# Gate columns of the expert layer: operands from VectorE and ScalarE alone, with more lag

## The chip, the cores and the metric

The kernel runs on one core of a Trainium2 chip. The metric is the device time of one execution in microseconds (us); lower is better. The engines are called as in the profile: PE is TensorE (matrix products), PEld its loading of stationary operands, DVE is VectorE, ACT is ScalarE, POOL is GpSimd, and SP starts DMA transfers.

## The reference

One encoder block over 1024 tokens of width 1024. A normalized input is projected to the queries, keys and values of a differential attention with 4 heads, to a short convolution, and to two gates; the gated sum is projected back and added to the input. Then comes a feed-forward layer over 16384 tiny experts, and a last normalization:

```
def chunk(xc):                       # PEER, product keys over 128 x 128 experts
    sc = einsum(q, sub_keys)         # 8 heads x 2 halves x 128 keys
    s1, i1 = top_k(sc[:, :, 0], 16); s2, i2 = top_k(sc[:, :, 1], 16)
    top, pos = top_k(all sums s1 + s2, 16)
    eidx = i1 * 128 + i2 at pos;  g = softmax(top)
    a = gelu(einsum(expert_u[eidx], xc))
    return einsum(g * a, expert_v[eidx])
```

So each token picks 8 x 16 = 128 experts, with a weight for each.

## The kernel before, in words

The tokens are 8 tiles of 128. Tiles 0 to 4 (group 0) meet all experts densely: PE multiplies every expert's `u` by the tokens, ACT applies gelu, DVE multiplies by a gate that is zero for experts not picked, and PE multiplies by `v`. Tiles 5 to 7 (group 1) fetch only the picked rows by indirect DMA (L739), and DVE works on them (L746, L755) beside the dense part.

The order of the program is: the projections of all tiles, then attention, gates and outputs of group 0, the key scores of group 0, and then the same stages (convolution, attention, mixing, scores) for group 1. Then comes the dense part over 128 blocks of 128 experts.

Two generators run beside the stages of group 1. The main program calls `tick(us)` after each group of matmuls with a rough time of its own; each generator then takes a step whenever its budget is used up (1.5 us of that time for `select_gen_all`, 1.6 us for `weights_gen`). So their instructions are spread among those of the main program, in the queue of each engine, at places that the program text fixes; a planner then orders the instructions of each engine by modelled times.

`select_gen` does the top-16 searches on DVE for one tile, twice (4 heads each). To read the picked key's index it compares positions with an iota (L637, DVE), multiplies the 0/1 result by the f32 indices `sf` (L639, POOL) and sums (L640, DVE).

`weights_gen` turns the picks of a tile of group 0 into dense gates. After three transposes the 128 picks lie on the 128 partitions, one token per column: `ib` holds the two key indices, `w` the weights. The gates of a token are then one matmul of two 128 x 128 one-hot matrices over the picks. A step handles WQ = 4 tokens: DVE compares the two indices with an iota in one instruction (`ms`, L714), POOL multiplies the first half by the weights into `o1` (L718), ACT casts the second half into `o2` (L720), PE multiplies (four matmuls with f32 operands, L695), and ACT copies the result into `wbuf` (L696). The operands lie in memory as [partition, token, key] and are written in the order key, token, so neighbours in the order of writing are 512 bytes apart. Each tile has 4 blocks of 8 steps; a block goes to DRAM in one transfer (`w_d`, L726). In all there are 160 steps and 20 transfers. The matmuls of a step are issued one step after its operands, but at the end of each block right behind them (L725). `ms`, `o1` and `o2` have WFB = 2 buffers. The results use two PSUM banks; the pool of these banks changes once, when the scores of group 0 are done.

The dense part reads the gates back (`wt`), so it needs all of `w_d` (`drain(wgt)`, L881). `mix` normalizes the rows of a group with a ring of `nt + MIXW` row buffers (`mixw`).

Of the kernel before, what the change touches and what calls it, by code (L numbers as in the profile page):

```python
# [49 lines left out]
WB = 4  # L50
WT = 32
WQ = 4
WFB = 2
GATHER = 2.0
SEL_STEP = 1.5
SEL_STEP_D = 8
# [9 lines left out]
def block_kernel(ctx, tc, x, wqkv, wcols, wpr, wo, wq, skT, uv, uT, an_w, fn_w, fin_w, sub_w,  # L66
# [7 lines left out]
    def pool(name, bufs=1, stack=None, **kw):  # L74
        return (stack or left).enter_context(tc.tile_pool(name=name, bufs=bufs, **kw))
# [448 lines left out]
    def mix(tt0, nt, c0, keep_hn, rings, mT, hnT, outer=None):  # L524
        with ExitStack() as st:
            if outer:
                st = outer
            wk = pool("mixw", nt + MIXW, stack=st)
            fn_b = rows_bcast(pool("mixn", stack=st), fn_w, D, "fn_b")
            xts = []  # L530
            for i in range(nt):
                tt = tt0 + i
                xts.append(row(wk, "xt2"))
                SP.dma_start(out=xts[i], in_=x[tt * P:(tt + 1) * P, :])
            later = []
            for j in range(2):
                w = units_k(rings[j], wo, j)
                for i in range(nt):
                    tt, xt = tt0 + i, xts[i]
                    ph = ps["g"].tile([P, 512], F32, name="ph2", tag="g")  # L540
                    gemm(ph, kts(mT, slice(c0 + i * P, c0 + (i + 1) * P)), w)
                    V.tensor_add(xt[:, j * 512:(j + 1) * 512], ph, xt[:, j * 512:(j + 1) * 512])
                    if j == 1:
                        SP.dma_start(out=h_d[tt * P:(tt + 1) * P, :], in_=xt)
                        hn = row(wk, "hn")
                        norm_rows(xt, fn_b, hn, hn, "h")
                        if keep_hn:
                            SP.dma_start(out=hn_d[tt * P:(tt + 1) * P, :], in_=hn)
                        if later:
                            transposes(*later.pop(0))  # L550
                        later.append((hn, hnT, c0 + i * P))
            if outer:
                return lambda: transposes(*later.pop(0))
            transposes(*later.pop(0))
# [39 lines left out]
    def select_gen(small, tt, ev, gw, done=None):  # L594
        hh = PH // 2
        sh = [P, hh, TOPK, TOPK]
        s3 = [P, hh, TOPK]

        t = small

        for a in range(2):
            sc = t([P, PH, NK], F32, "sc")
            SP.dma_start(out=sc, in_=sc_d[tt * P:(tt + 1) * P, a * PH * NK:(a + 1) * PH * NK]
                         .rearrange("p (h c) -> p h c", c=NK))
            sv, si = t([P, PH, TOPK], F32, "sv"), t([P, PH, TOPK], U32, "si")
            for hp in range(PH):
                top16(t, sc[:, hp, :], NK, sv[:, hp, :], si[:, hp, :])
                yield
            ohs = sc.rearrange("p h c -> p (h c)").bitcast(BF16).rearrange("p (j h a k) -> p j h a k", j=2, a=TOPK, k=TOPK)
            sf = t([P, PH, TOPK], F32, "sf")  # L610
            V.tensor_copy(out=sf, in_=si)
            svv = sv.rearrange("p (h q) k -> p h q k", q=2)
            sfv = sf.rearrange("p (h q) k -> p h q k", q=2)
            tv, ti = t(s3, F32, "tv"), t(s3, U32, "ti")
            cd = t([P, hh, CAND], F32, "cd")
            for c0, a0, na, nb in ((0, 0, 4, TOPK), (64, 4, TOPK - 4, 4)):
                sc2 = [P, hh, na, nb]
                V.tensor_tensor(out=cd[:, :, c0:c0 + na * nb].rearrange("p h (a b) -> p h a b", b=nb),
                                in0=svv[:, :, 0, a0:a0 + na].unsqueeze(3).broadcast_to(sc2),
                                in1=svv[:, :, 1, :nb].unsqueeze(2).broadcast_to(sc2), op=ALU.add)  # L620
            yield
            for h in range(hh):
                top16(t, cd[:, h, :], CAND, tv[:, h, :], ti[:, h, :])
                yield
            for j in range(2):
                pi, pj, pf = t(s3, U32, "pi"), t(s3, U32, "pj"), t(s3, BF16, "pf")
                if j == 0:
                    V.tensor_scalar(pi, ti, 4, None, op0=ALU.logical_shift_right)
                    V.tensor_scalar(pj, ti, 2, None, op0=ALU.logical_shift_right)
                    V.scalar_tensor_tensor(pf, pj, -12.0, pi, op0=ALU.add, op1=ALU.max)  # L630
                else:
                    V.tensor_scalar(pi, ti, 12, None, op0=ALU.bitwise_and)
                    V.tensor_scalar(pj, ti, 3, None, op0=ALU.bitwise_and)
                    V.scalar_tensor_tensor(pf, ti, 64.0, pi, op0=ALU.is_lt, op1=ALU.mult)
                    V.tensor_tensor(out=pf, in0=pf, in1=pj, op=ALU.add)
                oh = ohs[:, j]
                V.tensor_tensor(out=oh, in0=pf.unsqueeze(2).broadcast_to(sh), in1=iota_k.unsqueeze(1).broadcast_to(sh),  # L637
                                op=ALU.is_equal)
                PL.tensor_tensor(out=oh, in0=oh, in1=sfv[:, :, j, :].unsqueeze(3).broadcast_to(sh), op=ALU.mult)  # L639
                V.tensor_reduce(out=ev[j][:, a * 64:(a + 1) * 64].rearrange("p (h k) -> p h k", k=TOPK),  # L640
                                in_=oh.rearrange("p h a k -> p h k a"), axis=AX.X, op=ALU.add)
                yield
            dv = t(s3, F32, "dv")
            V.tensor_tensor(out=dv, in0=tv, in1=tv[:, :, 0:1].broadcast_to(s3), op=ALU.subtract)
            A.activation(tv, dv, AF.Exp)
            zz = t([P, hh], F32, "zz")
            V.tensor_reduce(out=zz, in_=tv, axis=AX.X, op=ALU.add)
            V.reciprocal(out=zz, in_=zz)
            V.tensor_tensor(out=gw[:, a * 64:(a + 1) * 64].rearrange("p (h k) -> p h k", k=TOPK), in0=tv,
                            in1=zz.unsqueeze(2).broadcast_to(s3), op=ALU.mult)  # L650
            if done:
                done(a * 64, (a + 1) * 64)
            yield
# [30 lines left out]
        yield from select_gen(t, tt, ev, gw, done)  # L684

    def weights_gen(wf):
        later = []
        iota_t = wf.tile([P, NK, WQ], BF16, name="iota_t", tag="iota_t", bufs=1)
        repeated_iota(wf, iota_t, "wtr")

        def finish(buf, q, o1, o2):
            for t in range(0, WQ, 4):
                pw = ps["w"].tile([P, 4, NK], F32, name="pw", tag="g")
                for u in range(4):
                    PE.matmul(pw[:, u, :], lhsT=o2[:, t + u, :], rhs=o1[:, t + u, :], start=True, stop=True)  # L695
                A.copy(out=buf[:, :, q + t:q + t + 4], in_=pw.rearrange("p t i -> p i t"))  # L696

        for c in range(NB):
            while c >= len(chosen):
                yield  # L700
# [5 lines left out]
            w = wf.tile([P, P], F32, name="wtr", tag="wtr", bufs=2)  # L706
            A.copy(out=w, in_=pt[:, 2, :])
            for b in range(P // WT):
                buf = wf.tile([P, NK, WT], F32, name="wbuf", tag="wbuf", bufs=1)
                for q in range(0, WT, WQ):  # L710
                    ts = slice(b * WT + q, b * WT + q + WQ)
                    sh = [P, NK, WQ]
                    ms = wf.tile([P, 2] + sh[1:], BF16, name="ms", tag="ms")
                    V.tensor_tensor(out=ms, in0=ib[:, :, ts].unsqueeze(2).broadcast_to([P, 2] + sh[1:]),  # L714
                                    in1=iota_t.unsqueeze(1).broadcast_to([P, 2] + sh[1:]), op=ALU.is_equal)
                    o1 = wf.tile([P, WQ, NK], F32, name="o1", tag="o1")
                    o2 = wf.tile([P, WQ, NK], F32, name="o2", tag="o2")
                    PL.tensor_tensor(out=o1.rearrange("p t i -> p i t"), in0=ms[:, 0],  # L718
                                     in1=w[:, ts].unsqueeze(1).broadcast_to(sh), op=ALU.mult)
                    A.copy(out=o2.rearrange("p t i -> p i t"), in_=ms[:, 1])  # L720
                    if later:
                        finish(*later.pop(0))
                    later.append((buf, q, o1, o2))
                    yield
                finish(*later.pop(0))  # L725
                A.dma_start(out=w_d[c * (P // WT) + b], in_=buf)  # L726

    def gather_gen(gat):
        st = {}
# [95 lines left out]
    with ExitStack() as pb:  # L825
# [7 lines left out]
        with ExitStack() as st:  # L833
# [18 lines left out]
            cfg.update(raw=raw, lo=PL)  # L852
            scores(2, NB - 2, 2 * P, (wring, wloc), hnT, sk)
            ready.update(range(2, NB))

    pa = ExitStack()
    ctx.push(pa)
# [185 lines left out]
```

## Time and profile before

| | |
|---|---|
| Runs (us) | 3186.97, 3195.77, 3201.72; median 3195.77 |
| The profiled execution | 3191.78 us, its span 3190.0 us |
| Mean granted TensorE clock | 0.978 |
| Busy over the span | PE 94%, PEld 87%, DVE 83%, ACT 41%, POOL 29% |
| Instructions | 45907 |
| Costliest groups | dense matmuls L905, indirect fetches L739, DVE on fetched rows L746 and L755 |
| L718 (POOL, `o1`) | 160 times, 203.0 us in all |

Times are from the profile of one execution. A group of instructions is shown with its line, engine, operation, the tiles it writes and reads, shapes, count, total and mean time, and then the idle time of the engine just before, with what ended it. Matmuls overlap each other, so their durations add up to more than the time that passes. A wait for several things is put down to the one that came last.

### The profile page before, as it was taken

To read this page: it belongs to the slowest core of one execution; us is meant where nothing else is said; L and a number is where in the kernel's file an instruction comes from. 1 tells how busy PE (TensorE), PEld (TensorE's weight loads), DVE (VectorE), ACT (ScalarE), POOL (GpSimd) and SP (SyncE) were. 2 spreads that over 40 slices of the span, in tenths; PEclk is the share of its full clock that TensorE was granted. 3 is DMA by queue.
4 is the path that set the end of the run, shared out by engine and by line. 5 is a ranking of instruction groups with operands and counts; after the bars stand their busy time and mean duration, and the time that the engine had idled before them with its cause. 6 is when DMAs were issued, how large, how long until landed. Compare 5 with 4: busy or idle time off the path is not lost.

```text
span 3190.0 us, 45907 instructions
## 1 busy us (share of the span) xinstructions
PE 3012.1 (94%) x17551; PEld 2761.0 (87%) x17551; DVE 2646.3 (83%) x4665; ACT 1302.9 (41%) x2344; POOL 923.5 (29%) x716
## 2 busy tenths in 40 slices
PE   7999999898989879799999999999999999999994
PEld 6799998798988869789989989899889999999993
DVE  5442466378999996799999999999999999999898
ACT  3322364335567766533333333333333333333332
POOL 2310000035344444223222222223332323333333
PEclk9999999999999989899999999999999999999997
DMA  5451232555444375779878888888889999898887
GB/s 180 145 182 67 83 113 80 199 172 213 146 172 157 144 260 196 255 249 333 316 277 321 316 299 309 295 316 293 313 328 343 340 341 348 326 347 325 328 336 281
DMA packets 237549, 801.11 MB, mean 251 GB/s; under 512 B 18832, under 2 KB 123280, under 8 KB 174096
## 3 DMA queue, kind: packets, MB, share of 16 engines
q0 software_dynamic: 64704, 442.53, 37.5%
q1 hardware_dynamic: 152592, 305.30, 27.8%
q10 hardware_dynamic: 20032, 50.34, 4.1%
q8 instruction: 138, 2.26, 0.3%
q14 instruction: 83, 0.68, 0.1%
HBM read 714.74 MB, written 83.36 MB: 250 GB/s over the span
## 4 chain that ended last, share of the span: by engine, by line
PE 56%; DVE 17%; issue 11%; DMA 8%; POOL 4%; ACT 3%; SPq 0%; ACTq 0%; POOLq 0%; DVEq 0%
PE z L905 17%; PE pout L905 10%; PE held L905 6%; PE pq L228 4%; PE pg L228 4%; POOL uvt L739 3%; PE ph L228 3%; DMA uvt<-in_uv,idx 3%; DVE acc L755 2%; PE py L228 2%; PE pw L695 2%; DVE uvt L746 2%; DVE ms L714 1%; PE pv L228 1%; PE pk L228 1%
## 5 line engine op out<-in xcount | busy, mean ns | idle before, releaser
L739 POOL DMA_INDIRECT uvt<-in_uv,idx x384 | 528.1, 1375 | 1288.5 <-DVE acc L755 1011.0
L905 PE MATMUL z<-actTh,uh 128*128 128x320 f32 x2048 | 636.3, 311 | 5.5 <-ACT pr L929 4.5
L905 PE MATMUL z<-actTh,uhl 128*128 128x320 f32 x2048 | 636.5, 311 | 1.1 <-DVE uhl L898 1.1
L905 PE MATMUL z<-actTl,uh 128*128 128x320 f32 x2048 | 635.3, 310 | 0.0
L746 DVE SCALAR_TENSOR_TENSOR uvt<-uvt,hng 128x1024 f32<-128x1024 f32 x384 | 468.0, 1220 | 41.1 <-DMA uvt<-in_uv,idx 40.3
L755 DVE SCALAR_TENSOR_TENSOR acc<-uvt,wt,acc 128x1024 f32<-128x1024 f32 x381 | 487.8, 1280 | 1.3 <-ACT wt L749 1.2
L905 PEld LDWEIGHTS z<-actTh,uh 128*128 128x128 f32 x2048 | 386.0, 188 | 20.5 <-ACT pr L929 8.6
L905 PEld LDWEIGHTS z<-actTl,uh 128*128 128x128 f32 x2048 | 386.2, 189 | 10.1
L905 PEld LDWEIGHTS z<-actTh,uhl 128*128 128x128 f32 x2048 | 386.8, 189 | 8.5 <-DVE uhl L898 2.2
L905 PE MATMUL pout<-vh,ph 128*128 128x512 f32 x768 | 302.5, 394 | 23.2 <-ACT ph L896 15.0
L905 PE MATMUL pout<-vhl,ph 128*128 128x512 f32 x768 | 301.1, 393 | 0.0
L905 PE MATMUL pout<-vh,phl 128*128 128x512 f32 x768 | 300.5, 391 | 0.0
L718 POOL TENSOR_TENSOR o<-ms,wtr 128x512 f32<-128x512 bf16 x160 | 203.0, 1311 | 262.1 <-PE pw L695 123.4
L748 ACT ACTIVATE wt<-zt 128x1 f32<-128x1 f32 x384 | 77.0, 201 | 493.3 <-DVE uvt L746 493.0
L957 DVE TENSOR_TENSOR hacc<-pout,hacc 128x512 f32<-128x512 f32 x384 | 259.4, 681 | 19.6 <-PE pout L905 19.1
L185 DVE TENSOR_TENSOR wl<-wr,wh 128x2048 fp32r<-128x2048 f32 x66 | 157.9, 2392 | 117.7 <-ACT wh L184 117.7
L896 ACT CAST uh<-raw 128x1024 fp32r<-128x1024 f32 x128 | 134.3, 1049 | 193.5 <-DMA raw<-in_uT 187.9
L184 ACT CAST wh<-wr 128x2048 fp32r<-128x2048 f32 x74 | 141.0, 1907 | 168.9 <-DMA wr<-in_wq 31.6
L695 PE MATMUL pw<-o,o 128*128 128x128 f32 x1280 | 169.1, 284 | 41.2 <-POOL o L718 17.6
L695 PEld LDWEIGHTS pw<-o,o 128*128 128x128 f32 x1280 | 161.1, 198 | 49.3 <-issue 25.6
L905 PE MATMUL held<-vhl,ph 128*128 128x512 f32 x512 | 199.6, 391 | 0.0
L720 ACT CAST o<-ms 128x512 f32<-128x512 bf16 x160 | 179.6, 1138 | 38.8 <-DVE ms L714 26.0
(290 smaller groups left out, 6673.5 us busy)
## 6 DMA issues: line engine op xcount, KB each, us to landing
raw<-in_uT SPq DMA_DIRECT2D x128, 512.0 KB
raw<-in_uv SPq DMA_DIRECT2D x128, 512.0 KB
w_d<-wbuf ACTq DMA_DIRECT2D x20, 2048.0 KB
wt<-w_d SPq DMA_DIRECT2D x32, 1280.0 KB
wr<-in_wcols SPq DMA_DIRECT2D x28, 1024.0 KB
wr<-in_wq SPq DMA_DIRECT2D x24, 1024.0 KB
xt<-in_x SPq DMA_DIRECT2D x16, 512.0 KB
q_d<-qt POOLq DMA_DIRECT2D x32, 256.0 KB
```

The source lines that it names most:

```text
L184: A.copy(out=op[0][sl], in_=src)
L185: lo.tensor_sub(op[1][sl], src, op[0][sl].bitcast(F32))
L228: PE.matmul(pd, lhsT=l[a], rhs=r[b], start=i == 0 and j == 0, stop=i == n - 1 and j == len(c) - 1)
L695: PE.matmul(pw[:, u, :], lhsT=o2[:, t + u, :], rhs=o1[:, t + u, :], start=True, stop=True)
L718: PL.tensor_tensor(out=o1.rearrange("p t i -> p i t"), in0=ms[:, 0], in1=w[:, ts].unsqueeze(1).broadcast_to(sh), op=ALU.mult)
L720: A.copy(out=o2.rearrange("p t i -> p i t"), in_=ms[:, 1])
L739: PL.indirect_dma_start(out=t[:], out_offset=None, in_=uv, in_offset=bass.IndirectOffsetOnAxis(ap=sels[c][1][:, k:k + 1], axis=0))
L746: V.scalar_tensor_tensor(u, u, 1.0, st[c], op0=ALU.mult, op1=ALU.mult, accum_out=zt)
L755: V.scalar_tensor_tensor(st["acc"], v, wt, st["acc"], op0=ALU.mult, op1=ALU.add)
L896: A.copy(out=hi, in_=t)
L905: PE.matmul(ps, lhsT=lhs[k][a], rhs=rhs[k][b], start=first and k == 0 and j == 0, stop=last and k == n - 1 and j == 2)
L957: V.tensor_add(hacc[:, t - NR, ds], ps, hacc[:, t - NR, ds])
```

## The change

- `weights_gen` makes each comparison by itself. `ms` is now the first comparison alone (DVE, bf16). The second comparison is written by DVE straight into `o2` (f32, in the key, token order). `o1` is made by ACT: four activations per step, one per token, each reading every fourth element of `ms` and multiplying by the weight of the pick as a per-partition scale. POOL has no part in it.
- `ms`, `o1` and `o2` have three buffers (WFB = 3).
- The matmuls of a step come two steps behind its operands (`made`), and the copy out of a result one more step behind (`done`). `flush()` finishes what is pending: after each tile, and once when the pool of PSUM banks changes.
- In `select_gen` the product with the indices goes to DVE, with `sf` in bf16.
- The second `mix` (group 1) has one row buffer less (2 instead of MIXW = 3 beside the tiles' own).

```
-WFB = 2
+WFB = 3
...
-            wk = pool("mixw", nt + MIXW, stack=st)
+            wk = pool("mixw", nt + (2 if tt0 else MIXW), stack=st)
...
-            sf = t([P, PH, TOPK], F32, "sf")
+            sf = t([P, PH, TOPK], BF16, "sf")
...
-                PL.tensor_tensor(out=oh, in0=oh, in1=sfv[:, :, j, :].unsqueeze(3).broadcast_to(sh), op=ALU.mult)
+                V.tensor_tensor(out=oh, in0=oh, in1=sfv[:, :, j, :].unsqueeze(3).broadcast_to(sh), op=ALU.mult)
...
+        def operands(c, b, q, ib, w):
+            ts = slice(b * WT + q, b * WT + q + WQ)
+            ms = wf.tile(sh, BF16, name="ms", tag="ms")
+            V.tensor_tensor(out=ms, in0=ib[:, 0, ts].unsqueeze(1).broadcast_to(sh), in1=iota_t, op=ALU.is_equal)
+            o2 = wf.tile([P, WQ, NK], F32, name="o2", tag="o2")
+            V.tensor_tensor(out=o2.rearrange("p t i -> p i t"), in0=ib[:, 1, ts].unsqueeze(1).broadcast_to(sh),
+                            in1=iota_t, op=ALU.is_equal)
+            o1 = wf.tile([P, WQ, NK], F32, name="o1", tag="o1")
+            for u in range(WQ):
+                A.activation(o1[:, u, :], ms[:, :, u], AF.Copy, scale=w[:, b * WT + q + u:b * WT + q + u + 1])
+            made.append((c, b, q, o1, o2))
+
+        def columns():
+            c, b, q, o1, o2 = made.pop(0)
+            pw = ps["w"].tile([P, WQ, NK], F32, name="pw", tag="g")
+            for u in range(WQ):
+                PE.matmul(pw[:, u, :], lhsT=o2[:, u, :], rhs=o1[:, u, :], start=True, stop=True)
+            done.append((c, b, q, pw))
+
+        def keep():
+            c, b, q, pw = done.pop(0)
+            if q == 0:
+                at["buf"] = wf.tile([P, NK, WT], F32, name="wbuf", tag="wbuf", bufs=1)
+            A.copy(out=at["buf"][:, :, q:q + WQ], in_=pw.rearrange("p t i -> p i t"))
+            if q == WT - WQ:
+                A.dma_start(out=w_d[c * (P // WT) + b], in_=at["buf"])
+
+        def flush():
+            while done:
+                keep()
+            while made:
+                columns()
+                keep()
...
                 for q in range(0, WT, WQ):
-                    ms = wf.tile([P, 2] + sh[1:], BF16, name="ms", tag="ms")
-                    V.tensor_tensor(out=ms, in0=ib[:, :, ts].unsqueeze(2).broadcast_to([P, 2] + sh[1:]),
-                                    in1=iota_t.unsqueeze(1).broadcast_to([P, 2] + sh[1:]), op=ALU.is_equal)
-                    PL.tensor_tensor(out=o1.rearrange("p t i -> p i t"), in0=ms[:, 0],
-                                     in1=w[:, ts].unsqueeze(1).broadcast_to(sh), op=ALU.mult)
-                    A.copy(out=o2.rearrange("p t i -> p i t"), in_=ms[:, 1])
-                    if later:
-                        finish(*later.pop(0))
-                    later.append((buf, q, o1, o2))
+                    operands(c, b, q, ib, w)
+                    if done:
+                        keep()
+                    if len(made) > 2:
+                        columns()
                     yield
-                finish(*later.pop(0))
-                A.dma_start(out=w_d[c * (P // WT) + b], in_=buf)
+            flush()
...
             scores(2, NB - 2, 2 * P, (wring, wloc), hnT, sk)
             ready.update(range(2, NB))
+            state["flush"]()
```

## Rows read from the trace of the kernel before

The columns of a row of groups: line, engine, operation, tile written <- tiles read, shapes, count | busy us, mean ns of one | idle time before, and what ended it.

**Rows 1.** The page, part 1: busy us (share of the span) x instructions.

```profile
PE 3012.1 (94%) x17551; PEld 2761.0 (87%) x17551; DVE 2646.3 (83%) x4665; ACT 1302.9 (41%) x2344; POOL 923.5 (29%) x716
```

**Rows 2.** Stretches: length, busy us (x instructions) by engine, granted clock, DMA share, GB/s.

```profile
700.00:800.00 100.00, 87.69 (x545) 86.01 (x544) 87.75 (x286) 53.46 (x75) 56.52 (x31) 0.93 0.53 186
800.00:1200.00 400.00, 351.66 (x2237) 329.51 (x2236) 379.08 (x971) 267.67 (x397) 169.35 (x133) 0.95 0.49 179
1000.00:1100.00 100.00, 88.92 (x596) 83.04 (x595) 97.28 (x243) 75.87 (x133) 40.23 (x34) 0.95 0.42 157
1200.00:1320.00 120.00, 115.80 (x798) 113.94 (x797) 83.92 (x194) 83.21 (x120) 49.92 (x39) 1.00 0.49 175
1320.00:3150.00 1830.00, 1797.12 (x9971) 1627.17 (x9969) 1723.77 (x2605) 626.74 (x1289) 544.45 (x392) 1.00 0.88 319
```

**Rows 3.** Stretches, line L714 (DVE) alone, then line L639 (POOL) alone.

```profile
800.00:1200.00 400.00, 81.40 (x106) 0.95 0.49 179
...
800.00:1200.00 400.00, 24.01 (x12) 0.95 0.49 179
700.00:1320.00 620.00, 40.08 (x20) 0.96 0.50 180
```

**Rows 4.** Waits of PE, 800 to 1200: total us, times, longest.

```profile
PE pw L695 <- POOL o L718: 11.7, 10, 2.0
PE pw L695 <- ACT wbuf L696: 10.9, 3, 9.2
...
PE pw L695 <- ACT o L720: 5.8, 7, 3.0
```

**Rows 5.** Timeline near 1006 us: start, us, engine, line.

```profile
1005.95 2.38 POOL L639 TENSOR_TENSOR sc<-sc,sf 128x1024 bf16<-128x1024 bf16 x1 [3.75 <-DVE rz L395]
...
1006.45 1.88 DVE L396 SCALAR_TENSOR_TENSOR rz<-rz,nlam,zs 128x1 f32<-128x1 f32 x1
```

**Rows 6.** Groups by form, DVE, 800 to 1200.

```profile
L714 DVE TENSOR_TENSOR ms<-ib,iota_t 128x1024 bf16<-128x1024 bf16 x106 | 82.4, 787 | 4.0 <-ACT o L720 2.9 <-POOL o L718 1.0
L185 DVE TENSOR_TENSOR wl<-wr,wh 128x2048 fp32r<-128x2048 f32 x22 | 56.1, 2548 | 6.5 <-ACT wh L184 6.5
...
L640 DVE TENSOR_REDUCE e<-sc 128x64 f32<-128x1024 bf16 x12 | 25.0, 2088 | 0.0
L397 DVE SCALAR_TENSOR_TENSOR p<-p,rz,p 128x1024 f32<-128x1024 f32 x12 | 18.1, 1507 | 0.1
...
L637 DVE TENSOR_TENSOR sc<-pf,iota_k 128x1024 bf16<-128x1024 bf16 x12 | 8.2, 679 | 0.1
...
L396 DVE SCALAR_TENSOR_TENSOR rz<-rz,nlam,zs 128x1 f32<-128x1 f32 x12 | 6.5, 538 | 0.0
```

**Rows 7.** Single lines, whole run: count, ns min/median/max, first and last start.

```profile
L714 DVE TENSOR_TENSOR ms<-ib,iota_t x160: 654/679/2030, 732.6 to 1313.4; 128x1024 bf16<-128x1024 bf16 x160
...
L185 DVE TENSOR_TENSOR wl<-wr,wh x66: 2268/2291/3779, 11.4 to 1287.6; 128x2048 fp32r<-128x2048 f32 x66
...
L397 DVE SCALAR_TENSOR_TENSOR p<-p,rz,p x32: 1259/1284/2124, 358.7 to 1082.0; 128x1024 f32<-128x1024 f32 x32
...
L396 DVE SCALAR_TENSOR_TENSOR rz<-rz,nlam,zs x32: 191/219/1916, 358.4 to 1080.1; 128x1 f32<-128x1 f32 x32
```

**Rows 8.** Groups by form, whole run, DVE and ACT.

```profile
L957 DVE TENSOR_TENSOR hacc<-pout,hacc 128x512 f32<-128x512 f32 x384 | 259.4, 681 | 19.6 <-PE pout L905 19.1
...
L720 ACT CAST o<-ms 128x512 f32<-128x512 bf16 x160 | 179.6, 1138 | 38.8 <-DVE ms L714 26.0 <-PE pw L695 9.2 <-issue 2.2
...
L196 ACT COPY dT<-pt 128x512 f32<-128x512 f32 x64 | 37.2, 592 | 10.8 <-PE pt L191 10.7
...
L449 ACT ACTIVATE at<-po,rz 128x128 f32<-128x128 f32 x32 | 12.0, 374 | 29.1 <-PE po L228 29.1
```

**Rows 9.** Timeline at 1290 us, DVE.

```profile
1290.10 1.28 DVE L714 TENSOR_TENSOR ms<-ib,iota_t 128x1024 bf16<-128x1024 bf16 x2
```

**Rows 10.** Chain that ended last, near 1328 us: start, us, what.

```profile
1328.05 19.98 DMA wt<-w_d
```

More of the change, by code (lines that the diff above doesn't have):

```diff
@@ L686, in weights_gen @@
     def weights_gen(wf):
-        later = []
         iota_t = wf.tile([P, NK, WQ], BF16, name="iota_t", tag="iota_t", bufs=1)
         repeated_iota(wf, iota_t, "wtr")
[L691 to L696, printed above, removed]
+        made, done, at = [], [], {}
+        sh = [P, NK, WQ]
+        def operands(c, b, q, ib, w):
[28 more added lines that the diff above has]
+                keep()
+        state["flush"] = flush
         for c in range(NB):
@@ L708, in weights_gen @@
             for b in range(P // WT):
-                buf = wf.tile([P, NK, WT], F32, name="wbuf", tag="wbuf", bufs=1)
                 for q in range(0, WT, WQ):
-                    ts = slice(b * WT + q, b * WT + q + WQ)
-                    sh = [P, NK, WQ]
-                    ms = wf.tile([P, 2] + sh[1:], BF16, name="ms", tag="ms")
-                    V.tensor_tensor(out=ms, in0=ib[:, :, ts].unsqueeze(2).broadcast_to([P, 2] + sh[1:]),
-                                    in1=iota_t.unsqueeze(1).broadcast_to([P, 2] + sh[1:]), op=ALU.is_equal)
-                    o1 = wf.tile([P, WQ, NK], F32, name="o1", tag="o1")
-                    o2 = wf.tile([P, WQ, NK], F32, name="o2", tag="o2")
-                    PL.tensor_tensor(out=o1.rearrange("p t i -> p i t"), in0=ms[:, 0],
-                                     in1=w[:, ts].unsqueeze(1).broadcast_to(sh), op=ALU.mult)
-                    A.copy(out=o2.rearrange("p t i -> p i t"), in_=ms[:, 1])
-                    if later:
-                        finish(*later.pop(0))
-                    later.append((buf, q, o1, o2))
+                    operands(c, b, q, ib, w)
[3 more added lines that the diff above has]
+                        columns()
                     yield
-                finish(*later.pop(0))
-                A.dma_start(out=w_d[c * (P // WT) + b], in_=buf)
+            flush()
     def gather_gen(gat):
```

## The prediction

> **What bounds the kernel now.** I read the busy line of the page first: PE is busy for 94% of the span, DVE for 83%, and one would call the kernel PE-bound [rows 1]. The change touches only part of the span, so the next view is the table of stretches [rows 2]. From 1320 to 3150 us (the dense part) PE is busy for 1797 of 1830 us and sets the pace. The comparisons of the gate columns start between 733 and 1313 us [rows 7], and there it is otherwise: from 800 to 1200 us DVE is busy for 379.1 of 400 us and PE for 351.7, at a mean granted clock of 0.95; in the hundred us from 1000 DVE reaches 97.28%. From 700 to 800 us DVE has 12 us to spare, from 1200 to 1320 us 36 us. So the stretch from 800 to 1200 decides, and in it DVE, not PE, is the fuller engine. Of the 160 steps (a step makes four gate columns) 106 lie there, and 12 of the POOL products of the selection [rows 3].
>
> The waits of PE in that stretch name the gate columns all the same: PE stands 28.4 us before their matmuls, 11.7 for POOL's `o1`, 10.9 for ACT's copy out and 5.8 for ACT's `o2` [rows 4]. These are what the change takes away. But POOL and ACT start when DVE's `ms` is there, so a wait for `o1` can be a DVE that is behind.
>
> **What DVE gets back.** POOL's products hold DVE up. At 1006 us a DVE operation on one element takes 1.88 us beside a POOL product of 2.38 us [rows 5]; its median is 0.219. I compare the means in the stretch [rows 6] with the medians of the whole run, which are mostly undisturbed [rows 7]: L714 106 x (0.787 - 0.679) = 11.4 us, L185 22 x (2.548 - 2.291) = 5.7, L396 12 x (0.538 - 0.219) = 3.8, L397 12 x (1.507 - 1.284) = 2.7; 24 us. The many smaller forms of that list, taken the same way, bring it to about 49 us. With L718 and L639 gone from POOL I credit 49, with 24 and 55 as ends.
>
> **What DVE is given, per step.** Now: one comparison of 1024 bf16, 0.679 undisturbed. After: two of 512. The bf16 one (`ms`) keeps the fixed part, which the one-element operation bounds at 0.19 [rows 7], and half the rest: 0.19 + (0.679 - 0.19) / 2 = 0.43 us. The other writes `o2` as f32 in the layout of the matmul, each element 512 bytes from the last. No DVE operation of this trace writes so. Below, the f32 addition of 512 elements takes 0.681 (L957). Above, ACT's cast L720, which writes exactly this pattern today, takes 1.138 where an ACT copy of 512 elements into contiguous places takes 0.592 (L196), a factor of 1.92 [rows 8]; on 0.681 that is 1.31. The nearest DVE row is the reduction L640, which reads its 1024 elements 32 bytes apart: 2.088, so 1.04 for 512 if all of it scales, 1.14 if 0.19 is fixed [rows 6]. I take 1.10. Neighbours overlap by 0.08: two L714 together take 1.28, not 1.36 [rows 9]. So a step costs DVE 0.43 + 1.10 - 0.08 - 0.679 = 0.77 us more, and 106 steps 82 us.
>
> [...]
>
> **Selection.** The product L639 goes from POOL to DVE: 12 in the stretch. One operand is repeated along the innermost index, which no row shows. [...] I take the dearer one: 12 x (1.284 - 0.08) = 14 us (below: 7). [...]
>
> **ACT.** One cast of 1.138 becomes four activations of 128 elements with a scale from SBUF; L449 is one, 0.374 [rows 8], so 1.50, 0.36 more. 106 x 0.36 = 38 us on 267.7 busy us of 400 [rows 2]: hidden as long as ACT is not full. Reading `ms` at every fourth element could cost as the strided write does, (1.138 - 0.592) / 512 = 1.07 ns an element, 0.55 a step, 58 us more: still below 440. On ACT's queue the copies out and the casts of weights stand behind these four; the extra step of lag covers that.
>
> **PE, buffers, DMAs.** The matmuls are as many and as long. Two more steps of lag and a third buffer let operands come later; the forced catch-up after every eighth step (20 times) becomes one after every 32nd (5) and one where the first PSUM pool closes. The transfers to `w_d` are the same 20 on ACT's queue. One row buffer less in the second mix: the third `hn` waits for the transposes of the first, which stand before it in PE's order; nothing (if it did wait, it would be for those transposes, a few us, once).
>
> **The sum.** From 800 to 1200 us DVE would be busy for 379.1 + 82 + 14 - 49 = 426 us. At the share that it reaches in its best hundred us, 0.973, that is 438 us: 38 more. PE's 28 us of waits are not saved there: the same PE work stands before a later DVE, and the waits move to the softmax maximum and to the columns. Outside it, the other 54 steps and 8 selection products add 42 + 10 us, less some 24 us of POOL's disturbance, to stretches with 48 us to spare; PE's waits for columns end there: 6 us gained (12 to -5). In the dense part the products of the three other token tiles, 4 each, add 12 x 1.2 = 14 us to a DVE with 106 us idle behind a PE with 33: nothing (if the cover fails, 14). At its start the first gate block is read back in 19.98 us [rows 10] after the last write; the last step's operands come about 2 us later (0.77 of DVE, 0.36 of ACT, two more copies out). Sum: 38 - 6 + 2 = 34 us. The profiled execution took 3191.8 us (its span 3190.0), so 3226; the median of the runs shown is 4 us above that execution: **3230 us**.
>
> **Rivals.**
> - *DVE writes `o2` at full rate (0.681).* [...] Place: the same stretch. 379 + 106 x (0.681 - 0.33) + 7 - 49 = 374 us of DVE, 385 us at 0.973, 15 saved, and 8 elsewhere: **3173**, faster. It decides from `o2` below 0.79 us, where the stretch with the other terms comes out even.
> - *Everything at its dear end.* `o2` at 1.31, only 24 us given back: 379 + 104 + 14 - 24 = 473, 486 us at 0.973, 86 more: **3282**. ACT's strided reads push the same way. For it: ACT shows just this write at this price.
> - *The bound doesn't move.* DVE's queue is full of work that PE needs only later (selection, columns two steps ahead), so the excess is worked off in the 36 idle us from 1200 to 1320 and PE keeps its pace: **3196**. Against: the softmax maxima L387 and the weights' low parts L185 stand in the same in-order queue.
>
> **Chances.** My forecast 0.44 (own range 3205 to 3255), the dear end 0.18, full-rate writes 0.22, no movement 0.16. The spread of the runs (3187 to 3202) allows 0.5%, 16 us, to be told from nothing. Faster is the full-rate case, 0.22; the same is the unmoved bound, 0.16; slower the rest, 0.62. Range: from just below 3173, the middle of the fast case, to just above the dear one: 3172 to 3285.
>
> **What would show it.** `o2` as a DVE group of 160 at about 1.1 us and `ms` at 0.43; L639 at about 1.28 on DVE; L396 back at 0.22; no DVE operation stretched beside POOL; no PE waits for `o1`. The stage from 700 to the first dense matmul would be some 34 us longer with DVE at 95% or more of its middle, and the dense part as long as before. I am wrong if `o2` takes less than 0.8, or if DVE falls below 90% there while the stage doesn't shrink (then ACT or the lag sets the pace).

## The result, and the profile after

The changed kernel takes 3236.34 us, median of four runs (3234.53 to 3238.88), beside 3198.74 us for the kernel before on the same chip (3186.97 to 3202.25): a ratio of 1.0128, 95% interval 1.0106 to 1.0150. The forecast was 3230 us. So it is slower, by 38 us, and the profiled execution is 46 us longer (its span 3236.2 us against 3190.0). Direction and size were right; several of the places were not, so the size is in part luck.

**The groups.** First the new or moved instructions, from 700 to 1400 us of the changed kernel (line, engine, operation, shapes, count | busy us, mean ns of one | idle before).

```profile
L697 DVE TENSOR_TENSOR o<-ib,iota_t 128x512 f32<-128x512 bf16 x160 | 168.9, 1069 | 12.9 <-PE pw L708 12.9
L695 DVE TENSOR_TENSOR ms<-ib,iota_t 128x512 bf16<-128x512 bf16 x160 | 74.2, 470 | 2.0 <-ACT o L701 1.8
L639 DVE TENSOR_TENSOR sc<-sc,sf 128x1024 bf16<-128x1024 bf16 x22 | 26.6, 1211 | 0.1
L397 DVE SCALAR_TENSOR_TENSOR p<-p,rz,p 128x1024 f32<-128x1024 f32 x12 | 15.4, 1280 | 0.0
L396 DVE SCALAR_TENSOR_TENSOR rz<-rz,nlam,zs 128x1 f32<-128x1 f32 x12 | 2.5, 211 | 0.0
```

```profile
L701 ACT ACTIVATE o<-ms,wtr 128x128 f32<-128x128 bf16 x640 | 208.7, 404 | 70.3 <-PE pw L708 46.0 <-DVE ms L695 22.3 <-PE ps L376 1.2
L715 ACT COPY wbuf<-pw 128x512 f32<-128x512 f32 x160 | 89.9, 577 | 29.0 <-DMA w_d<-wbuf 15.5 <-PE pw L708 13.4
```

On DVE the price list of the forecast held to within 0.07 us: `o2` 1.069 us (forecast 1.10), `ms` 0.470 (0.43), the selection product 1.211 (1.28), and the two rows that measured POOL's disturbance of DVE are back at their undisturbed times, L396 from 538 to 211 ns and L397 from 1507 to 1280 ns [rows 6]. The four activations cost ACT 1.62 us a step (forecast 1.50).

**The stretches** of the changed kernel (columns as in [rows 2]):

```profile
700.00:800.00 100.00, 77.43 (x462) 74.37 (x460) 87.83 (x266) 45.73 (x104) 21.49 (x7) 0.91 0.40 141
800.00:1200.00 400.00, 353.54 (x2188) 332.04 (x2189) 387.19 (x1048) 276.42 (x676) 9.52 (x12) 0.94 0.45 165
1000.00:1100.00 100.00, 85.07 (x578) 78.66 (x577) 99.54 (x231) 83.31 (x217) 5.78 (x7) 0.98 0.41 153
1200.00:1320.00 120.00, 105.12 (x667) 101.98 (x666) 103.69 (x240) 82.53 (x200) 2.59 (x3) 0.91 0.57 207
1320.00:1400.00 80.00, 57.47 (x321) 54.40 (x320) 72.73 (x240) 40.68 (x100) 4.32 (x4) 0.74 0.55 201
1400.00:3150.00 1750.00, 1743.97 (x9718) 1587.15 (x9717) 1648.67 (x2437) 602.04 (x1246) 516.52 (x366) 1.00 0.89 321
```

DVE's share from 800 to 1200 rose from 379.1 to 387.2 us, and to 99.5% in its best hundred [rows 2]. But PE was busy for 353.5 us there, against 351.7 before, with 2188 matmul records against 2237 [rows 2]: it lost little. It fell back where no loss was forecast: 77.4 against 87.7 us from 700 to 800, and 57.5 us of the 80 from 1320. ACT, at 276.4 of 400, was never full.

**The landmarks.** The same three lines of PE in both kernels, before first, then after (ns min/median/max, first and last start us): the transposes of the picks, the key scores, the first form of the dense matmuls.

```profile
L703 PE MATMUL ptw<-ident,e x15: 270/272/332, 722.2 to 1215.9; 128*128 128x128 f32 x15
L564 PE MATMUL pcs<-sk,qp x256: 270/275/579, 618.5 to 1314.1; 128*128 128x128 f32 x128
L905 PE MATMUL z<-actTh,uh x2048: 302/310/415, 1317.7 to 3122.7; 128*128 128x320 f32 x187
```

```profile
L732 PE MATMUL ptw<-ident,e x15: 272/273/477, 732.0 to 1267.9; 128*128 128x128 f32 x15
L564 PE MATMUL pcs<-sk,qp x256: 270/275/582, 617.4 to 1344.4; 128*128 128x128 f32 x128
L925 PE MATMUL z<-actTh,uh x2048: 302/310/637, 1380.7 to 3167.2; 128*128 128x320 f32 x187
```

Differences of these starts give the account of the 46 us: +10 when the first picks are transposed, before a single step; +30 at the last key score; +63 at the first dense matmul; +45 at the last one (3122.7 to 3167.2). So 10 us are lost ahead of the steps, 20 in the steps' stretch, 33 between the last score and the dense part, and 18 come back in the dense part, whose start no longer waits for its inputs (before, PE stood 15.0 us at one of its first `pout` matmuls, for ACT's `ph`). How the 53 us between the first picks and the dense part split at the last score is a matter of order, not of cause: kernel 3 below has its last score at 1318.1 us, only 4 us later than before, and its first dense matmul at 1380.5 all the same.

**The tail.** PE of the changed kernel after the last scores (start, us, engine, line, [idle before <- releaser]):

```profile
1342.88 1.16 PE L708 MATMUL pw<-o,o 128*128 128x128 f32 x8 [0.53 <-ACT wbuf L715]
1343.88 0.83 PE L564 MATMUL pcs<-sk,qp 128*128 128x128 f32 x6
...
1352.65 2.08 PE L708 MATMUL pw<-o,o 128*128 128x128 f32 x8 [0.56 <-ACT wbuf L715]
1366.31 3.78 PE L708 MATMUL pw<-o,o 128*128 128x128 f32 x16 [11.58 <-ACT wbuf L715]
...
1377.93 2.04 PE L708 MATMUL pw<-o,o 128*128 128x128 f32 x8 [1.09 <-DVE sv L591]
1380.65 0.64 PE L925 MATMUL z<-actTh,uh 128*128 128x320 f32 x1 [0.68 <-ACT wbuf L715]
```

and what ACT did in the longest of these waits:

```profile
1353.39 1.37 ACT L701 ACTIVATE o<-ms,wtr 128x128 f32<-128x128 bf16 x4
1363.54 1.04 ACT L916 CAST vh<-raw 128x1024 fp32r<-128x1024 f32 x1 [8.77 <-DMA raw<-in_uv]
1364.49 1.30 ACT L701 ACTIVATE o<-ms,wtr 128x128 f32<-128x128 bf16 x4
```

When the scores are done, ten steps are still open, and they end one after the other with nothing else for PE to do. In the middle ACT stands 8.77 us at a cast for the dense part whose transfer isn't there; the copy out and the activations of the next steps are queued behind it, and PE waits 11.58 us. The granted clock of these 80 us is 0.74 on the mean: 1.00 from 1320 to 1342 us, but 0.50 from 1352.6 to 1370.1, and eight matmuls take 2.08 us at 1352.65, where they took 1.16 at 1342.88. What lowered it isn't shown. The tail shows where the delay comes out, not what makes it: kernel 1 below, which loses nothing, has one too, 32 us from its last score to its first dense matmul, with a wait of 10.83 us for the same copy.

**PE's waits** of the changed kernel from 700 to 1400 us (total, times, longest):

```profile
PE pw L708 <- ACT wbuf L715: 44.8, 28, 11.6
PE pw L708 <- DVE o L697: 12.6, 8, 4.5
PE ptw L732 <- DVE e L640: 11.2, 2, 10.4
```

The waits for POOL's `o1` and ACT's `o2` of [rows 4] are gone, and the waits for the columns as a whole rose: in this longer stretch from 41.2 us to 63.7 (the idle time of the matmul group in either kernel). That the name is now the copy out does not say that the copy is the cause; the experiments had to.

### The profile page after: what moved, and what is told of

The parts are those of the page before. It is cut to its first block, busy times and chain, and to the rows that moved or that the text cites. A ratio compares the mean times of both kernels' runs of the same rounds, so it can differ in the third digit from the quotient of the medians.

```text
span 3236.2 us, 46187 instructions
## 1 busy us (share of the span) xinstructions
PE 3035.4 (94%) x17551; PEld 2786.4 (86%) x17551; DVE 2711.6 (84%) x4857; ACT 1331.8 (41%) x2822; POOL 672.8 (21%) x524
## 4 chain that ended last, share of the span: by engine, by line
PE 50%; DVE 21%; issue 15%; DMA 6%; POOL 6%; ACT 2%; SPq 0%; POOLq 0%; DVEq 0%; ACTq 0%
PE z L925 15%; PE pout L925 8%; PE held L925 6%; POOL uvt L758 6%; PE pq L228 4%; PE pg L228 4%; DVE o L697 3%; DMA uvt<-in_uv,idx 2%; PE py L228 2%; DVE wl L185 2%; PE ph L228 2%; DVE ms L695 1%; PE pv L228 1%; DVE e L640 1%; DMA wr<-in_wq 1%
## 5 line engine op out<-in xcount | busy, mean ns | idle before, releaser
L758 POOL DMA_INDIRECT uvt<-in_uv,idx x384 | 542.1, 1412 | 1446.8 <-DVE acc L774 961.5
L185 DVE TENSOR_TENSOR wl<-wr,wh 128x2048 fp32r<-128x2048 f32 x66 | 150.8, 2286 | 114.0 <-ACT wh L184 112.9
L708 PE MATMUL pw<-o,o 128*128 128x128 f32 x1280 | 186.3, 297 | 63.7 <-ACT wbuf L715 44.8
L708 PEld LDWEIGHTS pw<-o,o 128*128 128x128 f32 x1280 | 174.0, 208 | 77.0 <-ACT wbuf L715 58.6
L701 ACT ACTIVATE o<-ms,wtr 128x128 f32<-128x128 bf16 x640 | 208.7, 404 | 70.3 <-PE pw L708 46.0
L949 ACT ACTIVATE pr<-z 128x640 f32<-128x640 f32 x128 | 90.2, 704 | 341.1 <-PE z L925 314.4
L916 ACT CAST vh<-raw 128x1024 fp32r<-128x1024 f32 x128 | 130.1, 1047 | 165.2 <-PE pout L925 156.4
```

Source lines behind the costliest of these rows:

```text
L185: lo.tensor_sub(op[1][sl], src, op[0][sl].bitcast(F32))
L701: A.activation(o1[:, u, :], ms[:, :, u], AF.Copy, scale=w[:, b * WT + q + u:b * WT + q + u + 1])
L708: PE.matmul(pw[:, u, :], lhsT=o2[:, u, :], rhs=o1[:, u, :], start=True, stop=True)
L758: PL.indirect_dma_start(out=t[:], out_offset=None, in_=uv, in_offset=bass.IndirectOffsetOnAxis(ap=sels[c][1][:, k:k + 1], axis=0))
L916: A.copy(out=hi, in_=t)
```

## The experiments

Two theories at the start. **Load:** DVE has more work than before in the stretch that sets the end, so the time follows DVE's microseconds. **Coupling** (called lag in the later runs): the columns two steps behind and the copy one more make PE, ACT and the two PSUM banks wait for each other. Ratios are to the kernel before on the same chip, with 95% intervals; the numbers follow the labels (there is no 9). Diffs are to the changed kernel, those of 6 and 11 to the kernel before. None of the twelve is faster than the kernel before.

**1. The same number of elements, written side by side.** Only the access order of `o2` changes; the matmuls then read another arrangement, so this kernel does not make the right gates.

```
-V.tensor_tensor(out=o2.rearrange("p t i -> p i t"), ...
+V.tensor_tensor(out=o2.rearrange("p t i -> p (t i)").rearrange("p (i t) -> p i t", t=WQ), ...
```

> The changed kernel, with one thing altered: the second comparison writes its 512 f32 results one behind the other and not 512 bytes apart (same count, type, reader and tile; so the matmuls read another arrangement, and the gates are not the reference's). Theory load (DVE has too much work): L697 falls from 1.07 to about 0.68 us, 160 x 0.39 = 62 us of DVE vanish between 700 and 1380 us, and most of the 41 us lost comes back: ratio to the kernel before 0.995 to 1.003. Theory coupling (the lag makes PE wait for ACT's copies out of two PSUM banks): DVE's price matters little, ratio 1.009 or more, and PE's waits for the copy out stay near 45 us.

Measured: 1.0007 (0.9994 to 1.0019). The two groups of this kernel, 700 to 1400 us:

```profile
L697 DVE TENSOR_TENSOR o<-ib,iota_t 128x512 f32<-128x512 bf16 x160 | 111.4, 701 | 15.3 <-PE pw L708 15.2
L695 DVE TENSOR_TENSOR ms<-ib,iota_t 128x512 bf16<-128x512 bf16 x160 | 68.6, 434 | 5.3 <-ACT o L701 5.0 <-ACT ib L734 0.3
```

The two groups are 63.1 us shorter in sum (168.9 - 111.4 + 74.2 - 68.6). Neighbours on DVE overlap, so its time on these comparisons is less than the sum; the first two lines below have it, for the changed kernel and for this one (the third is of kernel 5):

```profile
700.00:1400.00 700.00, 230.92 (x320) 0.91 0.48 173
700.00:1400.00 700.00, 172.57 (x320) 0.94 0.53 191
700.00:1500.00 800.00, 308.97 (x1280) 0.92 0.48 170
```

58.3 us less of DVE brought 0.0121 of 3197, 39 us, with the lag untouched. Without the stretched-out write the changed kernel loses nothing that the runs can tell; load is right on the main point. That doesn't make the write the only thing that costs, as kernel 2 shows. The waits for the copy are nearly as long as in the changed kernel (39.3 us against 44.8), so that row was not the cause.

**2. The schedule alone, 3. the operands alone.** The second kernel has the lag and the third buffer, but POOL's product, ACT's cast and the selection on POOL as before; the third has the new operands and the selection on DVE, with the matmuls one step behind.

```
2: +PL.tensor_tensor(out=o1.rearrange("p t i -> p i t"), in0=ms[:, 0], ...)   (in operands())
   +A.copy(out=o2.rearrange("p t i -> p i t"), in_=ms[:, 1])
3: -                    operands(c, b, q, ib, w)
   +                    if later:
   +                        finish(*later.pop(0))
   +                    later.append((buf, q, o1, o2))
```

> The changed kernel's schedule (two steps of lag, copy out one more, three buffers for o1 and o2, two for ms, catch-up per tile) with the operands of the kernel before: one comparison of 1024 on DVE, the product on POOL, the cast on ACT, the selection product on POOL. Theory load: DVE has its old work, so no loss, and PE's waits for o1 may shrink: ratio 0.988 to 1.002. Theory coupling: the lag itself costs, ratio 1.008 or more.

> The kernel before's schedule (one step of lag, catch-up at each block, two buffers) with the changed kernel's operands: two comparisons on DVE, four activations on ACT, the selection product on DVE. Theory load: the loss is all there, ratio 1.010 to 1.018. Theory coupling: without the lag the loss is gone, 1.004 or less.

Measured: the schedule alone 1.0085 (1.0059 to 1.0111), the operands alone 1.0086 (1.0060 to 1.0112). Each loses 27 us, together they lose 41 (by the ratio). So the parts don't add. Kernel 2 came out as coupling expected, kernel 3 between the two expectations and nearer to load's: a schedule that the forecast credited with 6 us costs when it has the old operands. It is a parcel of lag, third buffer and one row buffer less in `mix`, which no run takes apart.

**4. The selection product back on POOL.**

```
-V.tensor_tensor(out=oh, in0=oh, in1=sfv[...], op=ALU.mult)
+PL.tensor_tensor(out=oh, in0=oh, in1=sfv[...], op=ALU.mult)
```

> The changed kernel with the selection product (and f32 indices) back on POOL. Theory load: 22 products of 1.21 us leave DVE in the stage, 25 us, of which POOL's disturbance takes back some 8: 10 to 18 us faster than the changed kernel, ratio 1.007 to 1.010. Theory coupling: no change, 1.012 to 1.015.

Measured: 1.0123 (1.0096 to 1.0150), no effect that the runs can tell, though the intervals could hide one of some 10 us. It isn't evidence against load, because DVE won little. The lines give the stretch from the first transposes of the picks to the first dense matmul, in the kernel before, the changed kernel and kernel 4 (columns as in [rows 2]):

```profile
722.20:1317.70 595.50, 530.65 (x3426) 505.30 (x3426) 528.19 (x1373) 397.17 (x581) 263.65 (x198) 0.96 0.50 181
732.00:1380.70 648.70, 555.61 (x3426) 525.45 (x3426) 606.39 (x1620) 433.47 (x1060) 22.66 (x19) 0.92 0.47 171
731.90:1379.50 647.60, 547.18 (x3417) 516.38 (x3417) 600.56 (x1594) 433.35 (x1059) 60.52 (x38) 0.93 0.47 171
```

From the changed kernel to kernel 4, 23.0 us of products (19 of the 22) left DVE in this stretch, but its busy time fell by 5.8 us only, 606.4 to 600.6, and the stretch by 1.1. POOL's disturbance took most of the rest back, more than the 8 us that were expected: L396 337 ns against 211, `o2` 1097 against 1069 (4.5 us over 160). The forecast's 14 us for this part from 800 to 1200 were right as a price; what they are worth as time the runs can't tell.

**5. and 6. Another form of the operands on DVE:** eight instructions a step, each compares an f32 iota with one index per partition (and multiplies by the weight), written side by side; ACT only copies out. With the lag (5) and in the order of the kernel before (6).

```
+V.tensor_scalar(o1[:, u, :], iota_t, ib[:, 0, k], w[:, k], op0=ALU.is_equal, op1=ALU.mult)
+V.tensor_scalar(o2[:, u, :], iota_t, ib[:, 1, k], None, op0=ALU.is_equal)
```

> The changed kernel with both operands made by DVE alone, one token at a time, into contiguous places: per step four comparisons of an f32 iota with a per-partition index and multiplied by the weight (o1), four without the product (o2); ACT only copies out. Theory load: eight instructions of about 0.20 us that overlap by 0.08 are 1.0 us a step where the two comparisons take 1.46; 74 us of DVE less than in the changed kernel, ratio to the kernel before 0.997 to 1.004. Theory coupling: 208 us of activations leave ACT's queue, so the copies out are never late and PE's waits for them fall from 45 to under 15 us; ratio 0.988 to 0.997.

> The kernel before (its schedule, two buffers, selection product on POOL) with the operands as in e5_scalars_with_lag. Theory load: DVE has 1.0 us a step where it has 0.74 now, 42 us more, and gets back 50 to 60 us of POOL's disturbance: ratio 0.990 to 1.000, and PE's waits for o1 and o2 of 30 us shrink. Theory coupling: without the lag there is nothing to lose, and it is faster than e5_scalars_with_lag by 0.3% or more.

Measured: 1.0352 (1.0331 to 1.0373) and 1.0299 (1.0276 to 1.0322). Both theories missed the numbers, because both rested on a price of 0.20 us that overlaps by another 0.08, an estimate of mine for a form that no run had shown. The groups of kernel 5:

```profile
L698 DVE TENSOR_SCALAR o<-iota_t,ib,wtr 128x128 f32<-128x128 f32 x640 | 223.9, 352 | 2.6 <-PE pw L706 2.5
L699 DVE TENSOR_SCALAR o<-iota_t,ib 128x128 f32<-128x128 f32 x640 | 178.0, 279 | 1.2 <-ACT ib L732 1.2
```

The sum of 401.9 us counts overlaps twice: of DVE's time the operands take 309.0 us, instead of the changed kernel's 230.9 (third and first line of the fence at kernel 1). With these sizes load is served: 78 us more of DVE, 0.0224 of 3197 or 72 us more of time.

**7. The copy out right behind its matmuls, 8. the steps closer together.**

```
7: -if done:
   -    keep()
    if len(made) > 2:
        columns()
   +    keep()
8: -W_STEP = 1.6
   +W_STEP = 1.2
```

> The changed kernel, but each copy out of PSUM stands right behind its matmuls and not a step later. Theory coupling: a bank comes free a step earlier, PE's waits for the copies fall from 45 to under 20 us and the ratio is 1.004 to 1.010. Theory load: as the changed kernel, 1.011 to 1.015.

> The changed kernel with the gate steps issued every 1.2 us of the program's own clock and not every 1.6, so that they end earlier in program order. If the 41 us between the last score matmuls and the first dense one come only of where the steps stand, they fall under 20 and the ratio is 1.000 to 1.008. Theory load: DVE has as much to do before the dense part, what leaves the end comes back in the middle, 1.010 to 1.016.

Measured: 1.0109 (1.0090 to 1.0129) and 1.0118 (1.0099 to 1.0136). In 7, PE's waits from 700 to 1400 us:

```profile
PE pw L708 <- ACT wbuf L715: 19.6, 13, 5.2
PE pw L708 <- DVE o L697: 19.5, 10, 6.8
```

The wait for the copy fell from 44.8 to 19.6 us, that for DVE rose from 12.6 to 19.5, and the time fell by about 6 us, which the intervals don't tell from nothing. A row of waits that loses more than half bought at most a part of the loss: the name on a wait was the last of several late things. In 8 the tail didn't shrink: its last score starts at 1344.6 us and its first dense matmul at 1390.2. So it isn't only where the steps stand that makes it; what does isn't shown (PE's waits there are put down to ACT's copy, 22.8 us).

**10. to 12. The stretch moved from DVE to TensorE.** `o2` is stored with the token innermost, DVE writes it side by side, and the weight load reads every fourth element; the computation stays whole. 10 is this on the changed kernel, 12 on kernel 3; 11 is the kernel before with both operands stored so.

```
-o2 = wf.tile([P, WQ, NK], F32, name="o2", tag="o2")
+o2 = wf.tile(sh, F32, name="o2", tag="o2")             (sh = [P, NK, WQ])
...
-PE.matmul(pw[:, u, :], lhsT=o2[:, u, :], ...
+PE.matmul(pw[:, u, :], lhsT=o2[:, :, u], ...
```

> The changed kernel, with o2 stored with the token innermost: DVE writes it to adjacent places, and TensorE's weight load reads it at every fourth element, so that the computation stays whole. Load: L697 falls from 1069 to about 701 ns, as in e1_o2_contiguous, and the ratio to the kernel before is 0.999 to 1.003, if TensorE reads the stretched-out operand at no cost. Lag: the same 1.0007 as e1_o2_contiguous. What tells here is TensorE: if its weight load (198 ns) or matmul (284 ns) gets longer by 0.2 us with the stride, 640 of them add 0.13 ms of busy time and the ratio is above 1.01.

> The kernel before, with o1 and o2 stored with the token innermost: POOL and ACT write to adjacent places, and TensorE reads both operands at every fourth element. DVE's work is untouched. Load: only what DVE gets back of POOL's disturbance counts, at most a few us; 0.997 to 1.001. Rival, that TensorE's waits for operands (POOL o 17.6 us, ACT o 12.6 us) set the time: the cast falls from 1.138 to about 0.6 us, the wait for ACT goes, and the ratio is 0.990 to 0.996. If TensorE pays for the stride: above 1.005.

> e3_operands_alone (operands by DVE and ACT with the order of the kernel before, 1.0086) with o2 stored with the token innermost, written to adjacent places and read by TensorE at every fourth element. Load: 63 us less of DVE, worth the same 39 us as between the changed kernel and e1_o2_contiguous: 0.995 to 0.998, faster than the kernel before. If the lag of two steps costs nothing by itself, the ratio is that of e10_o2_read_strided; if it costs its 0.4%, this kernel is 0.4% below e10_o2_read_strided.

Measured: 1.0285 (1.0265 to 1.0304), 1.0303 (1.0277 to 1.0329), 1.0269 (1.0251 to 1.0287). The third case of the first expectation: TensorE pays. Matmuls and weight loads of 11 (both operands stretched), then of 10 (the weights alone); each of the 640 f32 matmuls shows as two records:

```profile
L695 PE MATMUL pw<-o,o 128*128 128x128 f32 x1280 | 319.9, 417 | 7.9 <-ACT wbuf L696 4.3
L695 PEld LDWEIGHTS pw<-o,o 128*128 128x128 f32 x1280 | 307.8, 330 | 9.7 <-issue 4.9
```

```profile
L708 PE MATMUL pw<-o,o 128*128 128x128 f32 x1280 | 313.5, 396 | 18.5 <-ACT wbuf L715 17.4
L708 PEld LDWEIGHTS pw<-o,o 128*128 128x128 f32 x1280 | 307.8, 327 | 23.0 <-ACT wbuf L715 20.4
```

In the kernel before, the load took 198 ns and the matmul 284. These runs give a third finding: PE is as close to the bound as DVE. From kernel 1 to 10 DVE's part is the same (`o2` 707 ns against 701) and PE's group grows from 181.7 to 313.5 us; the time grows by 0.0278 of 3197, 89 us, so 0.67 us per us of PE. From kernel 1 to the changed kernel it was 0.67 per us of DVE (39 of 58.3), from there to kernel 5 0.92 (72 of 78). Kernel 11 waits only 7.9 us before these matmuls, against 41.2 in the kernel before, while PE itself takes longer, and it is 97 us slower: here the waits of a near-full engine were no sum that a change could cash in.

**13. The v tiles of group 1 on POOL's queue.** The traces showed transfers that the diff doesn't touch at another place. SP and POOL of the changed kernel, and below it of the kernel before:

```profile
611.15 2.08 SPq L368 DMA_DIRECT2D vk<-v_d  x2
659.28 0.33 SPq L603 DMA_DIRECT2D sc<-sc_d  x1
```

```profile
651.99 0.33 SPq L603 DMA_DIRECT2D sc<-sc_d  x1
655.74 0.80 SPq L368 DMA_DIRECT2D vk<-v_d  x2
```

The q and k tiles move likewise, on POOL's queue from 660 to 612 us. Between 620 and 640 us PE is busy for 12.97 us instead of 16.58 (first the changed kernel, then the one before; last three columns: granted clock, DMA share, GB/s):

```profile
620.00:640.00 20.00, 12.97 (x96) 12.58 (x94) 2.29 (x1) 3.94 (x7) 0.00 (x0) 0.91 1.04 410
```

```profile
620.00:640.00 20.00, 16.58 (x126) 16.15 (x125) 6.88 (x3) 8.18 (x11) 0.00 (x0) 0.93 0.84 314
```

```
-SP.dma_start(out=vks[h], in_=v_d[h])
+(PL if t0 else SP).dma_start(out=vks[h], in_=v_d[h])
```

> The changed kernel, with the loads of the v tiles of group 1 (vk) issued on POOL's queue, not on SP's. With the third buffer the planner puts the first two of these loads at 611 us, ahead of five loads of score weights in SP's queue; in the kernel before they stand behind them, at 656 us. Theory: the score weights come late behind them, the first scores are read back 7 us later (SP's load of sc at 659.28 against 651.99), and everything behind moves with it; without them ahead of the weights, the load of sc is back at 652 to 654 us, the first transposes of the gate picks at 735, and the ratio is 1.009 to 1.011. Rival: DVE's load sets the end anyway and takes up a shift of its start: the landmarks move, the time doesn't, 1.012 to 1.013. If the loads still start at 611 on POOL's queue and only share the bandwidth with the weights: landmarks as in the changed kernel, 1.012 to 1.013 too, and the trace shows which.

Measured: 1.0109 (1.0089 to 1.0128), but the trace shows the third case:

```profile
610.83 1.07 POOL L368 DMA_DIRECT2D vk<-v_d  x2
```

The loads still start at 611 us, beside the score weights, whose five loads start from 612.07 (from 600 to 700 us the DMA share is 0.66 at 235 GB/s, as in the changed kernel); the first read-back stands at 656.90 us, the first dense matmul where it was. So the choice of queue moved neither the loads nor the first dense matmul, and what the 7 us at 652 are worth at the end stays open. The shift is in every trace with the lag and the third buffer that keeps `ms` (the changed kernel, 1, 2, 4, 7, 8, 10) and in none of 3, 5, 6, 11 and 12; I take it that the larger buffer space moved the attention tiles to addresses that are free earlier, which no run proves. It isn't needed for the 10 us ahead of the steps: kernels 3 and 12 have these loads in their old place (at 658.4 and 658.1 us) and transpose their first picks at 732.4 and 731.8 us, as late as the changed kernel.

**What the lag costs.** Four pairs have the schedule with and without it: +27 us with the old operands (kernel 2 against before), +13 (the changed kernel against 3), +17 (5 against 6, which differ in the selection product too; kernel 4 saw no effect of that), +5 (10 against 12). The intervals of the second pair touch and those of the fourth overlap. It paid in none, but only the first pair shows the cost at the gate columns: there the stretch from the first picks to the first dense matmul grew from 595.5 to 629.9 us. In the other three it is, with the lag, 648.7 us against 648.1, 705.5 against 714.4 and 691.8 against 701.5, so as long or 9 to 10 us shorter. What these pairs lose arises, in the one traced execution of each kernel, behind the last dense matmul of PE, where DVE finishes the fetched rows of group 1. The last form of the `pout` matmuls and the sums of the fetched rows, in the changed kernel and then in kernel 3:

```profile
L925 PE MATMUL pout<-vh,phl x768: 387/389/628, 1405.9 to 3192.8; 128*128 128x512 f32 x192
L774 DVE SCALAR_TENSOR_TENSOR acc<-uvt,wt,acc x381: 1254/1277/1307, 1411.7 to 3226.5; 128x1024 f32<-128x1024 f32 x191
```

```profile
L905 PE MATMUL pout<-vh,phl x768: 387/389/628, 1402.3 to 3191.9; 128*128 128x512 f32 x192
L755 DVE SCALAR_TENSOR_TENSOR acc<-uvt,wt,acc x381: 1257/1278/1295, 1410.3 to 3215.4; 128x1024 f32<-128x1024 f32 x191
```

From the last `pout` matmul to the end of the span it is 43.4 us against 33.2, and 53.8 against 27.8 and 43.4 against 33.4 in the other two pairs (41.9 in the kernel before, but 30.6 in kernel 4, which has the lag). Why it differs isn't settled. In kernel 2 the moved loads, DVE's columns late beside POOL and the copy are mixed; how much each carries isn't settled either. Two kernels that would tell more were not run: kernel 3 with the side-by-side write of kernel 1, and one with a second `wbuf`.

## Why the prediction was right, and where not

- *DVE is the fuller engine and decides.* Right on the main point: kernel 1 is the changed kernel without the stretched write, and the loss is gone. Not the whole: PE, with 351.7 of the same 400 us, is near enough that its own microseconds count as much, as kernels 10 to 12 show. "DVE, not PE" was too sharp.
- *The costs per instruction.* Right: 1.069 for 1.10, 0.470 for 0.43, 1.211 for 1.28, L396 and L397 back at their medians. The 1.10 was an estimate from other rows; at hops of 512 bytes the trace has 1.069. The 1.284 of the selection term is L397's median [rows 7]; that the product, with an operand repeated, costs as much no run shows: it took 1.211.
- *ACT hidden.* Right: 276 of 400 us. Reading `ms` at every fourth bf16 costs little: 404 ns against 374 for the nearest row, L449 [rows 8], 0.12 us a step and not the 0.55 that was feared.
- *"That is 438 us: 38 more" from 800 to 1200.* DVE's load itself was forecast well: its terms come to 82 + 14 - 49 + 42 + 10 - 24 = 75 us for the whole of the steps, and from the first transposes to the first dense matmul its busy time rose by 78 (528.2 to 606.4), some of it search work that the longer stretch took in. (The 49 us of disturbance are about 40 when every form of that list is taken against its median.) What was mis-sized, in place and in size, is the time that this load costs. From 800 to 1200 PE nearly kept its pace: the steps were put off behind PE's other work, as the rival of the unmoved bound had it. But what was put off came back, in this kernel mostly after the last score, where the forecast had 2 us and the trace shows 33. Over the whole of the steps it is 53 us (63 - 10), where the forecast had 34. The rival named the mechanism and forgot the bill: of DVE's 36 idle us from 1200 to 1320, 20 were used (103.7 of 120 busy), and were not enough.
- *"6 us gained" by the lag.* As a total it is wrong in sign: 5 to 27 us lost in four pairs. Where the forecast placed it, at the columns, it is 34 us lost with the old operands, and with the new ones nothing or 9 to 10 us gained. The loss of these three pairs lies behind the dense matmuls, for which the forecast had no term.
- *Dense part 0.* The work is the same, but its start held 15 us of waiting before; 18 us of the late tail were made good there. The sum came out because this and the missed tail pull against each other; that is luck, not to the credit of the terms.
- *Nothing ahead of the steps.* Wrong: 10 us. Kernels 3 and 12 have them without the moved transfers, so these don't explain them. DVE beside POOL has a part: the copy of the iota takes 4.81 us in the changed kernel and 4.83 in 3, next to a POOL subtraction of 4.59 and 4.61, where it took 0.42 before, begun 0.02 us ahead of such a subtraction. How large that part is isn't shown.
- *The rivals.* Full-rate write: `o2` would have had to be below 0.79; at 0.70 (kernel 1) the time is that of before, not the 3173 forecast. Whether PE, right behind, or the schedule takes the difference is not shown. The dear end didn't happen: 1.31 for `o2` was too dark, and with only 24 us given back DVE's load would have risen by 100 us and not by 78.

## What to carry to other kernels

Where two engines are both near nine tenths busy in a stretch (before the change PE 530.7 and DVE 528.2 of 595.5 us), moving work from a third engine to either cost a large part of it in time (0.52 of the engine's added time from the kernel before to the changed one, 41 of 78 us, and 0.67 to 0.92 between kernels 1, 5, 10 and the changed one), whichever of the two it landed on; the waits that such a move removed were worth little. Count that added time as the engine's own busy time, not as a sum of durations that overlap, and count what the third engine gives back or takes: in kernel 4 a move of 23.0 us changed DVE's busy time by 5.8. Put the stretched side of a layout change where there is slack: here ACT had the slack to write at 512-byte hops; DVE (0.37 us more per step) and TensorE (0.13 us more per weight load) had not. And when work is put off, look for the place that needs all of it, here the first dense matmul: the bill is there, not in the stretch that is full.

## What the runs showed of the hardware that I had not expected

- TensorE's weight load of 128x128 f32 takes 327 ns (kernel 10) instead of 198 (before) when it reads every fourth element (16 bytes apart); the matmul beside it 396 instead of 284, and 417 when its moving operand is stretched as well (kernel 11). ACT's read of `ms` at every fourth bf16 (8 bytes apart) took 404 ns, against 374 for L449 [rows 8]. What in the step costs this isn't shown.
- A DVE comparison of 128 f32 with an operand that is one number per partition takes 279 ns with one such number and 352 with two (kernel 5), and these overlap: the 1280 take 309.0 us of DVE's time, 0.24 us each, where their durations add up to 401.9. I had taken 0.20 less 0.08 of overlap for both.
- The 512-byte hop costs engines unlike amounts on 512 f32: DVE 1.069 us against 0.701 side by side (kernel 1), ACT's cast 1.138 [rows 8] against 0.62 (kernel 11), POOL's product a median of 1.13 (before) against 1.04 (kernel 11).
